# Order of the run-up to sparse attention in a two-layer decoder trunk on one core: compressed-block inner layer in quarters, query norms in halves

## The chip, the cores and the metric

One core of one Trainium2 chip runs the whole program. The metric is device microseconds of one execution, the median of several; lower is better. Engines are named as in the profile: PE (TensorE), PEld (its weight loads), DVE (VectorE), ACT (ScalarE), POOL (GpSimd), SP (SyncE, which issues nearly all transfers).

## What is computed

Two decoder layers on 512 tokens of width 1024. Layer 0 is a retention and mLSTM mixer, layer 1 a sparse attention; a gated MLP with a short convolution and a gated input embedding follow each. The change touches layer 1's attention alone, cut here to what matters:

```python
q = rms_norm(q.reshape(B, T, G, HG, HD), q_g)
def compress(t, pos, w1, w2):
    blk = kv(t)[:, cidx] + pos[:, None, :]
    return jax.nn.gelu(blk @ w1) @ w2
kc = rms_norm(compress(kc, pos_k, w1k, w2k), k_g[0])
vc = compress(vc, pos_v, w1v, w2v)
s = einsum(qq, kc) * scale ; p_c = softmax(s) ; o_cmp = p_c @ vc
p_s = softmax(selected keys)  ; o_slc = p_s @ selected values
p_w = softmax(window keys)    ; o_win = p_w @ window values
o = g0 * o_cmp + g1 * o_slc + g2 * o_win
h = h + o @ w_out ; h = h + conv_ffn(h) ; h = h + gate * rms_norm(p @ ple_w)
```

## The kernel before

Every weight is cut in two float parts, high (`wh`, made by ACT) and low (`wl`, made by DVE), after a 512 KB transfer into `wr`; a product is three matmuls with 512 columns (`mm3`, lines 161 to 163), high by high, low by high, high by low. `load` (line 145) takes each of its three tiles from three buffers in turn: a load's tile waits for the matmuls that read that buffer last, three loads earlier. PSUM has eight banks: four of tag "a", three of "b", one of "o".

The run-up stands at the end of `nsa_mixer`, written out by hand:

- `thin` makes the inputs of the compressed blocks (`hT`) and the gates. `Tokens.steps(c0, c1)` makes the c-th quarter of a product over all tokens: one load and 24 matmuls into four "a" banks. There are three such products: `kv` (keys and values), `q0` (heads 0 to 7), `q1` (heads 8 to 15).
- `blocks` adds positions to `hT` and splits the sums (tiles `xf` and, split, `pt`), for keys on DVE, for values on POOL. `hidden` multiplies them by `w1` in four loads of 16 rows each (lines 803 to 806, eight matmuls of 256 columns a load), adds the halves and applies GELU; `hidden_t` turns the result, `second` multiplies by `w2`, `cmp_keys` norms, `cmp_values` spreads.
- `kv_evac` empties the four `kv` banks; `key_stack` turns one token block of keys (8 transposes, line 772).
- `q_copy` empties two `q` banks (line 869); `q_sums` squares (line 878) and sums (line 880); `q_factor` makes the root by three Newton rounds (lines 204 to 206); `q_norm` multiplies by it (line 902) and splits (lines 896, 900); `q_stack_t` turns four blocks for one head (line 907).
- `Compressed` is the softmax over the compressed blocks for four heads: products (line 930), masked, maxima, shift, exp, factors, scaled, turned.

In source order: `kv` whole, key `hidden` whole, `q0` half, key stacks 0 and 1, `q0` rest with stacks 2 and 3, `q_norm`s, value `hidden` whole, `q1` in pieces, the first four query stacks, `q1` end, `second` for values, first `Compressed` up to its shift. Then 96 attention steps follow (`seq`: 16 heads by 6 units), each a score unit, the probabilities of four steps earlier and the values of two more; a planner (`fits`, `then`) puts other jobs in steps by estimated costs (`PACE` ns a step) and due times: the rest of the first `Compressed`, the squares of `q1`'s queries on POOL (from step 3), the embedding products (`EMBED_AT`).

```python
with tile.TileContext(nc, schedule_with_timeline_sim=True) as tc:
    trunk_kernel(tc, ins, out)
```

This context fixes each engine's queue at build time. It takes instructions by source order as far as they are ready by its own estimates, loads' work ahead (`high_priority`, line 151), so an engine's queue differs from the source. On the chip each queue runs in its order.

Of the kernel before, what the change touches and what calls it, by code (L numbers as in the profile page):

```python
# [20 lines left out]
P = 128  # L21
# [12 lines left out]
LAG, VALUES_LAG, OUT_WAIT = 4, 2, 3  # L34
LAST_AT = (100, 102)
PACE, SLACK = 1800, {"T": 2500, "V": 1000, "S": 1000, "G": 1500}
# [24 lines left out]
class Trunk:  # L61
# [608 lines left out]
    def nsa_mixer(self):  # L670
# [4 lines left out]
        with ExitStack() as ctx:  # L675
# [118 lines left out]
            def hidden(which, xs):  # L794
                ph = self.ps("b")
                for c in range(4):
                    hi, lo = self.load(I["w1"][which, c])
                    for q in range(4):
                        jj = 4 * c + q
                        ws = slice(256 * q, 256 * q + 256)  # L800
                        x = xs[c // 2][:, jj % 8]
                        if jj:
                            nc.tensor.matmul(ph[0:64, 0:256], x[:, 0], lo[:, ws], start=False, stop=False)
                        nc.tensor.matmul(ph[:, 0:256], x.rearrange("p a s -> p (a s)"), hi[:, ws], start=jj == 0, stop=jj == 15)
                        if jj == 0:
                            nc.tensor.matmul(ph[0:64, 0:256], x[:, 0], lo[:, ws], start=False, stop=False)
# [6 lines left out]
            def hidden_t(hid, times):  # L813
# [3 lines left out]
                hh, hl = [self.y()[:, 0 : P * times].rearrange("p (x r b) -> p x r b", x=4, b=32) for _ in range(2)]  # L817
# [70 lines left out]
            def q_norm(zq, r, t, sts, eng):  # L888
                z = zq[t // 2][:, t % 2].rearrange("p (h d) -> p h d", h=8)
                halves = []  # L890
                sts.append(halves)

                def high():
                    halves.extend(self.y().rearrange("p (h a d) -> p h a d", h=4, a=2) for _ in range(2))
                    for c, st in enumerate(halves):
                        nc.scalar.activation(st[:, :, 0], z[:, 4 * c : 4 * c + 4], AF.Copy)

                def low():
                    for c, st in enumerate(halves):
                        eng.tensor_tensor(st[:, :, 1], z[:, 4 * c : 4 * c + 4], st[:, :, 0].bitcast(F32), ALU.subtract)  # L900

                return [lambda: eng.tensor_tensor(z, z, r[:, 8 * t : 8 * t + 8].unsqueeze(2).to_broadcast([P, 8, 64]), ALU.mult), high, low]
# [598 lines left out]
```

## Time and profile before

| | |
|---|---|
| median of 3 runs | 1378.37 us (1378.05 to 1379.83) |
| profiled execution | 1380.31 us, span 1378.6 us, 17917 instructions |
| PE busy | 1361.5 us, 99% of the span |
| DVE, ACT, POOL busy | 832.8, 629.2, 393.9 us |
| run-up, 680 to 780 us | between `kv`'s last quarter and the first attention steps |

The span runs from the first to the last instruction; 1.7 us of the execution lie around it. A row of the timeline gives start, length, engine, line, tile names and, in brackets, idle time before it and what ended that. Matmul lengths overlap: what one costs is the distance between two starts.

### The profile page before, as it was taken

What the parts mean: (1) busy time and instruction counts of PE and PEld (TensorE: products, weight loads), DVE (VectorE), ACT (ScalarE), POOL (GpSimd) and SP (SyncE); (2) the same over time, 40 slices, a digit from 0 to 9 for tenths busy, and PEclk for the clock granted to TensorE, in tenths of its full rate; (3) what the DMA queues carried; (4) which work ended last, traced back from release to release, by engine and by line L of the source; (5) the groups of instructions that cost most, each with busy time, mean ns of one, the idle gap of its engine ahead of it and who ended that gap; (6) DMA issues with size and microseconds to landing.
All of it is one profiled execution on the core that took longest, in us unless ns stands there. A gap on an engine that the chain in (4) does not pass through costs nothing.

```text
span 1378.6 us, 17917 instructions
## 1 busy us (share of the span) xinstructions
PE 1361.5 (99%) x6702; PEld 1123.8 (82%) x6702; DVE 832.8 (60%) x1294; ACT 629.2 (46%) x1086; POOL 393.9 (29%) x392
## 2 busy tenths in 40 slices
PE   9999999999999999999999899999999999999998
PEld 6888788888888888888777678888888888888887
DVE  6765756566356435558766878865766346535555
ACT  5357426444224323336454688774444224313332
POOL 3355502122032101131420696754122022101120
PEclk9999999999999999999999999999999999999999
DMA  6533233233322332233343222012432323233232
GB/s 219 160 93 93 91 107 107 87 97 99 100 92 92 104 95 88 84 123 116 90 142 108 73 74 55 17 50 65 154 107 92 98 97 97 92 100 95 81 110 74
DMA packets 44096, 135.05 MB, mean 98 GB/s; under 512 B 5348, under 2 KB 5988, under 8 KB 44008
## 3 DMA queue, kind: packets, MB, share of 16 engines
q1 hardware_dynamic: 43720, 133.76, 31.2%
q8 instruction: 53, 0.87, 0.3%
q14 instruction: 35, 0.29, 0.1%
q10 hardware_dynamic: 288, 0.14, 0.0%
HBM read 124.69 MB, written 5.25 MB: 94 GB/s over the span
## 4 chain that ended last, share of the span: by engine, by line
PE 91%; DVE 3%; ACT 3%; issue 1%; POOL 1%; DMA 1%; SPq 0%; POOLq 0%; ACTq 0%
PE ps L161 27%; PE ps L163 27%; PE ps L162 26%; PE ps L1037 3%; PE ps L1012 2%; PE ps L981 1%; PE ps L982 1%; PE ps L391 1%; POOL acc L219 1%; DVE wl L134 1%; ACT pr L986 0%; PE ps L256 0%; PE ps L248 0%; PE ps L983 0%; PE ps L459 0%
## 5 line engine op out<-in xcount | busy, mean ns | idle before, releaser
L133 ACT ACTIVATE wh<-wr 128x1024 fp32r<-128x1024 f32 (+2 forms) x216 | 223.3, 1036 | 459.2 <-PE ps L162 366.8
L161 PE MATMUL ps<-y,wh 128*128 128x512 f32 (+1 forms) x1112 | 431.7, 390 | 0.2 <-ACT wh L133 0.2
L162 PE MATMUL ps<-y,wh 128*128 128x512 f32 (+1 forms) x1112 | 430.4, 388 | 0.0
L163 PE MATMUL ps<-y,wl 128*128 128x512 f32 (+1 forms) x1112 | 429.3, 389 | 0.3 <-DVE wl L134 0.3
L134 DVE TENSOR_TENSOR wl<-wr,wh 128x1024 fp32r<-128x1024 f32 (+2 forms) x199 | 246.0, 1237 | 99.3 <-ACT wh L133 98.7
L163 PEld LDWEIGHTS ps<-y,wl 128*128 128x128 f32 x1112 | 208.7, 188 | 44.0 <-DVE wl L134 0.7
L161 PEld LDWEIGHTS ps<-y,wh 128*128 128x128 f32 x1112 | 208.8, 188 | 43.6 <-ACT wh L133 0.7
L162 PEld LDWEIGHTS ps<-y,wh 128*128 128x128 f32 x1112 | 208.9, 188 | 41.8
L1285 POOL TENSOR_TENSOR sc<-sc,rb 128x512 f32<-128x512 f32 x44 | 58.9, 1338 | 469.0 <-ACT sc L1284 469.0
L219 POOL TENSOR_TENSOR acc<-acc,sc 128x512 f32<-128x512 f32 x48 | 75.0, 1562 | 233.4 <-ACT sc L217 230.2
L161 PE MATMUL ps<-gh,wh 128*128 128x512 f32 x352 | 136.9, 389 | 0.0
L162 PE MATMUL ps<-gl,wh 128*128 128x512 f32 x352 | 136.6, 389 | 0.0
L163 PE MATMUL ps<-gh,wl 128*128 128x512 f32 x352 | 136.3, 389 | 0.0
L1300 DVE TENSOR_TENSOR hp<-hp,ps 128x512 f32<-128x512 f32 x48 | 33.0, 687 | 128.3 <-PE ps L163 128.3
L1278 DVE TENSOR_TENSOR a<-ps,rb 128x512 f32<-128x512 f32 x44 | 30.3, 690 | 84.7 <-PE ps L163 84.7
L997 POOL TENSOR_SCALAR pr<-pr,sm,gate 128x512 f32<-128x512 f32 (+3 forms) x128 | 76.8, 619 | 16.5 <-DVE sm L995 11.4
L163 PEld LDWEIGHTS ps<-gh,wl 128*128 128x128 f32 x352 | 66.1, 188 | 13.8
L162 PEld LDWEIGHTS ps<-gl,wh 128*128 128x128 f32 x352 | 66.1, 188 | 13.8
L161 PEld LDWEIGHTS ps<-gh,wh 128*128 128x128 f32 x352 | 66.1, 188 | 13.6
L1286 DVE TENSOR_TENSOR sc<-ps,sc 128x512 f32<-128x512 f32 x44 | 30.3, 688 | 69.1 <-POOL sc L1285 63.9
L986 ACT ACTIVATE pr<-ps,nmx 128x512 f32<-128x512 f32 (+3 forms) x128 | 67.7, 540 | 7.4 <-DVE nmx L984 6.6
L1247 DVE TENSOR_TENSOR pt<-ps,pt 128x512 fp32r<-128x512 f32 (+1 forms) x96 | 56.5, 595 | 19.7 <-ACT pt L1015 19.3
(298 smaller groups left out, 1998.6 us busy)
## 6 DMA issues: line engine op xcount, KB each, us to landing
wr<-in_w_up_dram SPq DMA_DIRECT2D x88, 512.0 KB, 3.6
wr<-in_w_down_dram SPq DMA_DIRECT2D x32, 512.0 KB, 3.5
wr<-in_w_plg_dram SPq DMA_DIRECT2D x16, 512.0 KB, 3.5
wr<-in_w_down_dram SPq DMA_DIRECT2D x16, 384.0 KB, 3.1
hp<-in_xT_dram SPq DMA_DIRECT2D x16, 256.0 KB, 4.1
wr<-in_w_abo_dram SPq DMA_DIRECT2D x8, 512.0 KB, 3.6
wr<-in_w_dram SPq DMA_DIRECT2D x8, 512.0 KB, 3.7
wr<-in_w_q_dram SPq DMA_DIRECT2D x8, 512.0 KB, 3.6
```

Of the source, the lines that this page charges most:

```text
L133: self.nc.scalar.activation(hi, src, AF.Copy)
L134: (eng or self.nc.vector).tensor_tensor(lo, src, hi.bitcast(F32), ALU.subtract)
L161: mm(out, ah, bh, start=first, stop=False)
L162: mm(out, ah, bl, start=False, stop=False)
L163: mm(out, al, bh, start=False, stop=last)
L219: eng.tensor_tensor(n.acc, n.acc, sq, ALU.add)
L986: nc.scalar.activation(pr[:, b], s[:, b], AF.Exp, bias=nmx[:, b : b + 1], accum_out=sm[:, bs[b] : bs[b] + 1])
L997: nc.gpsimd.tensor_scalar(prs[b], prs[b], sm[:, b : b + 1], gate[:, j, hd, 1 + b : 2 + b], ALU.mult, ALU.mult)
L1037: nc.tensor.matmul(po[0:m, cols], vv[i][:, b, g, 0:m], src, start=False, stop=last and b == 1 and i == 0 and part == 0)
L1247: nc.vector.tensor_tensor(*lows, ALU.subtract)
L1285: nc.gpsimd.tensor_tensor(c, c, n.b, ALU.mult)
L1300: nc.vector.tensor_tensor(self.h[m], self.h[m], ps, ALU.add)
```

## The change

The key `hidden` becomes four `hidden_step`s, two among `kv`'s quarters, two among `q0`'s; the value one becomes two pairs around `q1`'s first quarter. Its bank is "o" in place of "b". The normed queries of `q0` get their squares from ACT, straight from PSUM (new line 876 in `q_copy`), in place of DVE; their norms go by halves of four heads, all token blocks of the first half first. Key stacks and the first query stacks move behind the norms. The first `Compressed` goes ahead of `q1`'s second half, and its `exp`, `factors` and `scaled` leave the step planner. The split output of `hidden_t` lies in a `pr` buffer in place of `y`. The first three embeddings take a "b" bank and are copied by DVE in place of ACT. `PACE` is 1950 in place of 1800; the planner looks for room for `q1`'s squares from step 5 in place of 3.

```diff
+Q1_AT = 5
-PACE, SLACK = 1800, ...
+PACE, SLACK = 1950, ...
@@ hidden @@
-            def hidden(which, xs):
-                ph = self.ps("b")
-                for c in range(4):
-                    hi, lo = self.load(I["w1"][which, c])
...
+            def hidden_step(which, xs, ph, c):
+                hi, lo = self.load(I["w1"][which, c])
+                for q in range(4):
...
+            def hidden(ph):
                 hid = self.sc()
@@ q_copy @@
+                    if ss is not None:
+                        sq = self.sc()
+                        nc.scalar.activation(sq, ps[i], AF.Square, scale=r)
+                        nc.vector.tensor_reduce(ss[:, 8 * t : 8 * t + 8], ..., AX, ALU.add)
@@ the run-up @@
-            kv.steps(0, 4)
+            kv.steps(0, 2)
             xk = blocks(0, hT[0])
+            kv.steps(2, 3)
+            ph = self.ps("o")
+            hidden_step(0, xk, ph, 0)
+            kv.steps(3, 4)
+            hidden_step(0, xk, ph, 1)
             keys = kv_evac(kv.ps)
             gate_columns(sg)
-            hk = hidden(0, xk)
             xv = blocks(1, hT[1])
             q0 = self.Tokens(self, I["w_q"][0], n)
-            q0.steps(0, 2)
-            key_stack(0, keys[0])
-            key_stack(1, keys[1])
+            q0.steps(0, 1)
+            hidden_step(0, xk, ph, 2)
+            q0.steps(1, 2)
+            hidden_step(0, xk, ph, 3)
+            hk = hidden(ph)
+            q0.steps(2, 3)
             hkt = hidden_t(hk, 1)
-            q0.steps(2, 3)
-            key_stack(2, keys[2])
-            key_stack(3, keys[3])
             q0.steps(3, 4)
+            zq = [q_copy(q0.ps[0:2], 0, ss), q_copy(q0.ps[2:4], 2, ss)]
+            for f in root + [f for c in range(2) for t in range(NTT) for f in q_norm(zq, r, t, sts, nc.vector, c)]:
+                f()
             po = second(0, *hkt)
             st = cmp_keys(po)
-            ...
-            hv = hidden(1, xv)
+            key_stack(0, keys[0])
+            ph = self.ps("o")
+            hidden_step(1, xv, ph, 0)
+            hidden_step(1, xv, ph, 1)
+            key_stack(1, keys[1])
             q1 = self.Tokens(self, I["w_q"][1], n)
-            q1.steps(0, 2)
-            hvt = hidden_t(hv, 4)
-            cmp_keys_t(st)
-            q1.steps(2, 3)
+            q1.steps(0, 1)
+            key_stack(2, keys[2])
+            hidden_step(1, xv, ph, 2)
+            hidden_step(1, xv, ph, 3)
+            hv = hidden(ph)
+            key_stack(3, keys[3])
             for hd in range(4):
                 q_stack_copy(hd, q_stack_t(sts, hd, "b"))
+            q1.steps(1, 2)
+            cmp_keys_t(st)
+            comp = Compressed(0, "b")
+            for f in (products, masked, comp.maxima, comp.shift, comp.exp, comp.factors, comp.scaled):
+                f()
+            with self.behind(nc.tensor):
+                hvt = hidden_t(hv, 4)
+                q1.steps(2, 3)
+            cmp_values(second(1, *hvt))
             q1.steps(3, 4)
-            cmp_values(second(1, *hvt))
-            comp = Compressed(0, "b")
```

Where the queues change at the places that the prediction speaks of:

DVE at the last quarter of `kv` (before; `wl_903` and `wl_906` are `kv`'s quarters 2 and 3, counted from 0, `wl_923` is the first quarter of the key `w1`, `xf` the position sums):

```order
L134 TENSOR_TENSOR wl_903_5318<-wr_901_5316,wh_902_5317 128x1024
L715 TENSOR_TENSOR sc_885_5221<-ps_874_5138,rb_883_5214 128x512
L715 TENSOR_TENSOR sc_886_5223<-ps_878_5169,rb_883_5214 128x512
L134 TENSOR_TENSOR wl_906_5348<-wr_904_5346,wh_905_5347 128x1024
L789 TENSOR_TENSOR xf_907_5376<-sc_885_5221,cols_76 64x8x31
L185 TENSOR_TENSOR sc_890_5247<-sc_890_5247,ps_889_5230 64x512
L789 TENSOR_TENSOR xf_907_5376<-sc_885_5221,cols_76 64x8x31 x7
L722 TENSOR_TENSOR sc_890_5247<-sc_890_5247,rb_883_5214 48x512
L134 TENSOR_TENSOR wl_923_5456<-wr_921_5454,wh_922_5455 128x1024
```

The same place now (`wl_906` is quarter 2, `wl_910` the first of `w1`, `wl_913` is `kv`'s quarter 3; lines are those of the changed file):

```order
L135 TENSOR_TENSOR wl_906_5335<-wr_904_5333,wh_905_5334 128x1024
L716 TENSOR_TENSOR sc_885_5221<-ps_874_5138,rb_883_5214 128x512
L716 TENSOR_TENSOR sc_886_5223<-ps_878_5169,rb_883_5214 128x512
L135 TENSOR_TENSOR wl_910_5366<-wr_908_5364,wh_909_5365 128x1024
L790 TENSOR_TENSOR xf_901_5316<-sc_885_5221,cols_76 64x8x31
L186 TENSOR_TENSOR sc_890_5247<-sc_890_5247,ps_889_5230 64x512
L790 TENSOR_TENSOR xf_901_5316<-sc_885_5221,cols_76 64x8x31 x7
L723 TENSOR_TENSOR sc_890_5247<-sc_890_5247,rb_883_5214 48x512
L135 TENSOR_TENSOR wl_913_5380<-wr_911_5378,wh_912_5379 128x1024
```

`kv`'s quarter 3 and the first quarter of `w1` have changed places around the position sums.

ACT at the value `hidden` (before; `wh_1001` is the last quarter of the value `w1`, `wh_1009` to `wh_1030` the four quarters of `q1`):

```order
L133 ACTIVATE wh_1001_5871<-wr_1000_5870 128x1024
L133 ACTIVATE wh_1009_5893<-wr_1008_5892 128x1024
L133 ACTIVATE wh_1012_5923<-wr_1011_5922 128x1024
L808 ACTIVATE sc_1003_5884<-ps_990_5827 64x256
L133 ACTIVATE wh_1019_5964<-wr_1018_5963 128x1024
L810 ACTIVATE sc_1003_5884<-sc_1003_5884 64x256
L133 ACTIVATE wh_1030_6022<-wr_1029_6021 128x1024
```

And now (`wh_1002` and `wh_1005` are the third and fourth quarter of the value `w1`, `wh_1020` is `q1`'s second quarter, the `y` rows are high parts of normed queries, line 896 before):

```order
L134 ACTIVATE wh_1002_5877<-wr_1001_5876 128x1024
L911 ACTIVATE y_966_5701<-ep_957_5663 128x4x64
L911 ACTIVATE y_967_5705<-ep_960_5672 128x4x64
L911 ACTIVATE y_968_5709<-ep_960_5672 128x4x64
L134 ACTIVATE wh_1005_5891<-wr_1004_5890 128x1024
L911 ACTIVATE y_969_5713<-ep_957_5663 128x4x64
L911 ACTIVATE y_970_5717<-ep_957_5663 128x4x64
L134 ACTIVATE wh_1020_5955<-wr_1019_5954 128x1024
```

The query norms now stand among these splits; they stood behind them.

DVE at the first attention steps (before; `sc_1034` is the first `Compressed`, `nmx` the maximum of a score unit, `vc` the compressed values):

```order
L861 TENSOR_TENSOR sc_1033_6064<-ps_1032_6051,sc_1033_6064 128x64
L863 TENSOR_TENSOR vc0_5114<-sc_1033_6064,rows4_5116 128x512
L861 TENSOR_TENSOR sc_1033_6064<-ps_1032_6051,sc_1033_6064 128x64
L935 TENSOR_TENSOR sc_1034_6071<-ps_1037_6074,maskc_5038 128x256
L863 TENSOR_TENSOR vc1_5115<-sc_1033_6064,rows4_5116 128x512
L936 TENSOR_TENSOR sc_1034_6071<-sc_1034_6071,ps_1037_6074 128x256
L935 TENSOR_TENSOR sc_1034_6071<-ps_1038_6083,maskc_5038 128x256
L984 TENSOR_REDUCE nmx_1050_6120<-ps_1053_6123 128x1
L936 TENSOR_TENSOR sc_1034_6071<-sc_1034_6071,ps_1038_6083 128x256
L984 TENSOR_REDUCE nmx_1055_6137<-ps_1057_6139 128x1
```

And now (`tiny_1047` are sums of squares of `q1`, whose squares POOL makes; `y_1059` is the first embedding):

```order
L863 TENSOR_TENSOR sc_1035_6070<-ps_1034_6057,sc_1035_6070 128x64
L865 TENSOR_TENSOR vc0_5114<-sc_1035_6070,rows4_5116 128x512
L863 TENSOR_TENSOR sc_1035_6070<-ps_1034_6057,sc_1035_6070 128x64
L865 TENSOR_TENSOR vc1_5115<-sc_1035_6070,rows4_5116 128x512
L888 TENSOR_REDUCE tiny_1047_6126<-sc_1094_6267 128x8
L888 TENSOR_REDUCE tiny_1047_6126<-sc_1101_6293 128x8
L888 TENSOR_REDUCE tiny_1047_6126<-sc_1108_6320 128x8
L1000 TENSOR_REDUCE nmx_1050_6129<-ps_1053_6132 128x1
L1372 COPY y_1059_6158<-ps_1054_6138 128x512
L888 TENSOR_REDUCE tiny_1047_6126<-sc_1119_6364 128x8
L1000 TENSOR_REDUCE nmx_1055_6145<-ps_1057_6147 128x1
```

`Compressed` is gone from here (it stands before `q1`'s third quarter); three sums of squares stand ahead of the first score maximum, and an embedding copy behind it.

## Rows read from the trace of the kernel before

**Rows 1.** The page's head: span, and busy time of the engines

```profile
span 1378.6 us, 17917 instructions
PE 1361.5 (99%) x6702; PEld 1123.8 (82%) x6702; DVE 832.8 (60%) x1294; ACT 629.2 (46%) x1086; POOL 393.9 (29%) x392
```

**Rows 2.** Stretches: length, busy PE, PEld, DVE, ACT, POOL, granted clock, DMA share, GB/s

```profile
690.00:700.00 10.00, 9.12 (x47) 7.55 (x48) 8.21 (x21) 5.58 (x7) 0.00 (x0) 1.00 0.61 208
...
720.00:730.00 10.00, 7.40 (x40) 5.94 (x39) 9.61 (x17) 5.24 (x11) 0.00 (x0) 0.89 0.45 129
730.00:740.00 10.00, 10.00 (x43) 7.90 (x42) 9.64 (x38) 5.03 (x13) 0.00 (x0) 0.94 0.50 160
...
760.00:770.00 10.00, 8.91 (x48) 6.10 (x45) 9.93 (x29) 8.50 (x25) 7.45 (x11) 1.00 0.25 91
770.00:780.00 10.00, 6.80 (x38) 5.33 (x36) 8.38 (x17) 5.18 (x12) 8.74 (x9) 0.83 0.27 79
...
800.00:960.00 160.00, 159.01 (x1102) 133.03 (x1101) 114.02 (x249) 117.32 (x333) 106.39 (x143) 1.00 0.18 49
```

**Rows 3.** PE's timeline at its three losses; in brackets idle before, and its end

```profile
690.82 0.33 PE L803 MATMUL ps<-wl,pt 128*64 128x256 f32 x1 [2.14 <-DVE wl L134]
...
725.60 0.33 PE L803 MATMUL ps<-wl,pt 128*64 128x256 f32 x1 [1.28 <-DVE wl L134]
...
775.12 0.45 PE L981 MATMUL ps<-hp,y 128*128 128x384 f32 x1 [2.45 <-DVE y L913]
```

**Rows 4.** PE's timeline, `kv`'s last quarter: first and last of its 24 matmuls

```profile
680.65 0.39 PE L161 MATMUL ps<-wh,y 128*128 128x512 f32 x1
...
685.87 0.39 PE L163 MATMUL ps<-wh,y 128*128 128x512 f32 x1
```

**Rows 5.** DVE's timeline: splits of `w1`'s first and second quarter

```profile
681.98 1.21 DVE L134 TENSOR_TENSOR wl<-wr,wh 128x1024 fp32r<-128x1024 f32 x1
...
689.54 1.22 DVE L134 TENSOR_TENSOR wl<-wr,wh 128x1024 fp32r<-128x1024 f32 x1
```

**Rows 6.** PE's timeline: 16 matmuls of `hidden`, first and last; eight transposes

```profile
707.66 1.04 PE L772 MATMUL ps<-ident,st 128*128 128x128 f32 x8
...
720.41 0.28 PE L803 MATMUL ps<-wl,pt 128*64 128x256 f32 x1
...
722.11 0.28 PE L804 MATMUL ps<-wh,pt 128*128 128x256 f32 x1
```

**Rows 7.** ACT's timeline: two weight splits, eight query splits, two copies

```profile
658.13 2.01 ACT L133 ACTIVATE wh<-wr 128x1024 fp32r<-128x1024 f32 x2 [2.19 <-PE ps L162]
...
734.96 2.57 ACT L896 ACTIVATE y<-ep 128x256 fp32r<-128x256 f32 x8
...
746.62 0.58 ACT L915 ACTIVATE y<-ps 128x512 fp32r<-128x512 f32 x1
747.09 0.27 ACT L853 ACTIVATE kc<-ps 128x128 fp32r<-128x128 f32 x1
```

**Rows 8.** DVE's groups by shape, 655 to 790 us: busy us, mean ns, idle before

```profile
L863 DVE TENSOR_TENSOR vc<-sc,rows 128x512 fp32r<-128x512 f32 x2 | 3.6, 1822 | 0.0
...
L913 DVE CAST y<-ps 128x512 fp32r<-128x512 f32 x4 | 2.8, 689 | 5.2 <-PE ps L907 5.2
...
L935 DVE TENSOR_TENSOR sc<-ps,maskc 128x256 f32<-128x256 f32 x4 | 1.6, 412 | 0.0
L936 DVE TENSOR_TENSOR sc<-sc,ps 128x256 f32<-128x256 f32 x4 | 1.5, 408 | 0.0
```

**Rows 9.** DVE's timeline: a Newton operation, twice; POOL's: a weight split

```profile
732.60 0.26 DVE L204 TENSOR_TENSOR tiny<-tiny 128x32 f32<-128x32 f32 x2
...
772.20 1.81 DVE L204 TENSOR_TENSOR tiny<-tiny 128x32 f32<-128x32 f32 x1
...
771.61 2.36 POOL L143 TENSOR_TENSOR wl<-wr,wh 128x1024 fp32r<-128x1024 f32 x1
```

**Rows 10.** POOL's groups by shape, 655 to 790 us: squares of `q1`

```profile
L878 POOL TENSOR_TENSOR sc<-ep 128x512 f32<-128x512 f32 x4 | 4.9, 1262 | 0.0
```

More of the change, by code (lines that the diff above doesn't have):

```diff
@@ L34 @@
 LAG, VALUES_LAG, OUT_WAIT = 4, 2, 3
+Q1_AT = 5
 LAST_AT = (100, 102)
-PACE, SLACK = 1800, {"T": 2500, "V": 1000, "S": 1000, "G": 1500}
+PACE, SLACK = 1950, {"T": 2500, "V": 1000, "S": 1000, "G": 1500}
 EMBED_AT = (0, 1, 2, 6, 12, 17, 22, 27)
@@ L886, in q_factor, with q_norm, scaled @@
                 return r, [mean] + root + [scale]
[L888 removed]
+            def q_norm(zq, r, t, sts, eng, half=None):
+                cs = (0, 1) if half is None else (half,)
                 z = zq[t // 2][:, t % 2].rearrange("p (h d) -> p h d", h=8)
[L890 to L891 removed]
+                hs = slice(4 * cs[0], 4 * cs[-1] + 4)
+                if t == len(sts):
+                    sts.append([None, None])
+                def scaled():
+                    rb = r[:, 8 * t + hs.start : 8 * t + hs.stop].unsqueeze(2).to_broadcast([P, hs.stop - hs.start, 64])
+                    eng.tensor_tensor(z[:, hs], z[:, hs], rb, ALU.mult)
                 def high():
[L894 to L895 removed]
+                    for c in cs:
+                        st = sts[t][c] = self.y().rearrange("p (h a d) -> p h a d", h=4, a=2)
                         nc.scalar.activation(st[:, :, 0], z[:, 4 * c : 4 * c + 4], AF.Copy)
                 def low():
[L899 removed]
+                    for c in cs:
+                        st = sts[t][c]
                         eng.tensor_tensor(st[:, :, 1], z[:, 4 * c : 4 * c + 4], st[:, :, 0].bitcast(F32), ALU.subtract)
[L902 removed]
+                return [scaled, high, low]
             def q_stack_t(sts, hd, tag):
@@ L1122, in nsa_mixer @@
             ew = [self.load(I["w_ple"][1, 0])]
-            seq = [(hd, *u) for hd in range(16) for u in UNITS]
             todo, load = defaultdict(list), {e: defaultdict(int) for e in "TVSG"}
@@ L1192, in embed @@
                 got = []
-                then(s0, ("T", 1360, lambda: got.append(emb.products(m, ew[m // 4]))), ("S", 600, lambda: emb.keep(m, got[0])))
+                then(s0, ("T", 1360, lambda: got.append(emb.products(m, ew[m // 4], "b" if s0 < LAG else "a"))), ("V" if s0 < LAG else "S", 650, lambda: emb.keep(m, got[0], s0 < LAG)))
             def out_first(m, s0):
@@ L1199, in nsa_mixer @@
             wo = {}
-            for step, e, n, f in ((0, "S", 630, comp.exp), (1, "V", 1100, comp.factors), (2, "G", 1050, comp.scaled), (4, "T", 440, comp.turned), (5, "S", 600, comp.high), (6, "V", 690, comp.low)):
+            for step, e, n, f in ((1, "T", 440, comp.turned), (2, "S", 600, comp.high), (3, "V", 690, comp.low)):
                 load[e][step] += n
@@ L1208, in nsa_mixer @@
                 a, b = q_sums(zq, ss1, t, nc.gpsimd)
-                last = max(last, then(3 + t, ("G", 1050, a), ("V", 690, b)))
+                last = max(last, then(Q1_AT + t, ("G", 1050, a), ("V", 690, b)))
             for k in (0, 4, 7):
@@ L1330, in inputs, with products @@
             self.p = [x.rearrange("p (k t) -> p k t", k=2) for x in self.k.load(self.k.I["pT"][self.i])]
-        def products(self, m, w):
-            ps = self.k.bank()
+        def products(self, m, w, tag=None):
+            ps = self.k.ps(tag) if tag else self.k.bank()
             for k in range(2):
```

47 lines of the change are left out of this document (24 added, 23 removed).

## The prediction

> **What bounds the kernel.** The page's head first: PE is busy 1361.5 of 1378.6 us [rows 1], and the change keeps PE's instructions, 6746 matmuls before and after. So it can gain only time in which PE stands still or runs below its full clock, and these lie, for the places that the change touches, between 685 and 780 us. The stretches show them [rows 2]: PE idle 10.00 − 7.40 = 2.60 in 720 to 730, 10.00 − 8.91 = 1.09 in 760 to 770, 10.00 − 6.80 = 3.20 in 770 to 780. With the 2.14 before 690.82 [rows 3] that is 9.03 us. The clock is granted at 0.89, 0.94 and 0.83 in three stretches of 10 us [rows 2], at 1.2 GHz for a part of them and 2.4 for the rest: (0.11 + 0.06 + 0.17) × 10 = 3.4 us of full-speed work. It falls behind the losses near 725 and 775; after the 2.14 at 690 it stays 1.00 [rows 2, 3]. In all **12.4 us**. Behind 800 us PE idles 0.99 in 160 us [rows 2], so nothing is to be had there.
>
> The bracketed waits say why [rows 3]. Two follow a low split of a `w1` quarter on DVE (2.14, 1.28): in `hidden` a load feeds only eight matmuls, while a quarter of `kv` feeds 24 at (685.87 − 680.65)/23 = 0.227 us, 5.4 us [rows 4]. Sixteen matmuls of `hidden` take (722.11 − 720.41) × 16/15 = 1.8 [rows 6], 0.9 for a load, less than the 1.21 of one low split on DVE [rows 5]. Four such loads in a row outrun DVE, and the change puts each one or two between longer pieces. The third wait is 2.45 for the copy of a query stack (line 913) at the loop's start, where DVE is busy 9.93 + 8.38 = 18.3 of 20 us [rows 2, 3].
>
> **The change part by part.**
>
> *Removed: 12.4 us.* The two `w1` waits go, since the rows that fed them no longer stand together; the loop-start wait goes as far as DVE is relieved there (D). The clock's 3.4 goes if no loss of the size of those at 725 and 775 comes back.
>
> *A: `kv`'s quarter 3, +1.6.* Its low split stands on DVE behind the position sums, where the first `w1` split stood (order above). Thus it starts about 681.98 and ends at 683.19 [rows 5]. PE starts that quarter's high products about 680.65 and wants its low part at the fifth matmul, 680.65 + 4 × 0.227 = 681.56 [rows 4]. Wait 683.19 − 681.56 = 1.6. Behind the split on DVE stand the second `w1` split and the evacuations of `kv`; PE then has 16 matmuls of `hidden` and the rest of `kv` before it wants the banks, which covers them. Bounds 0 (if DVE reaches it early) and 1.6.
>
> *B: query splits among weight splits on ACT, +1.2.* From the third value load to `q1`'s second quarter, ACT holds three weight splits of 1.0 (2.01 for two) and five query splits of 2.57/8 = 0.32 [rows 7]: 4.6 us. PE has meanwhile two loads of `hidden` at 0.9 and twelve transposes at 1.04/8 = 0.13 [rows 6], 3.4 us. The difference is 1.2. If all eight query splits come late it is 3.0 + 2.57 − 3.4 = 2.2; if they are done early, 0. I take the middle because the order has five of them between.
>
> *C: `Compressed` ahead of `q1`'s second half, +0.6.* Its first product waits on ACT for a weight split (1.0), a stack copy (0.58) and `kc` (0.27) [rows 7], 1.85 us, against ten transposes at 0.13 [rows 6], 1.3. The difference is 0.6; without that cover 1.9, and 0 if the split is early. In exchange the shift and exponentials lie under 48 matmuls.
>
> *D: the loop's start, +1.2 in place of 1.09 + 3.20 = 4.3.* DVE's queue there loses the two `vc` spreads, 3.6, which come earlier, and half of eight maskings, (1.6 + 1.5)/2 = 1.6 [rows 8]; it gains three embedding copies, priced as the copy of a 128x512 bank at line 913, 3 × 0.69 = 2.1 [rows 8]. Relief 3.1, so 4.3 − 3.1 = 1.2 stays. Bounds 0 and 4.3: whether the relief falls before the late copy, no row shows.
>
> *At nothing.* The squares of `q0` on ACT add four operations there and take four from DVE; they run bank by bank while PE makes 6 × 0.227 = 1.4 us of products for each bank [rows 4], and one copy takes 0.58 [rows 7], two 1.2. If that cover fails, `q1`'s first quarter waits for a bank, some tenths of a us, within B's bounds. The `pr` buffer, the "o" bank and the norm by halves change places alone. Loads keep their number; DMA is at most 0.61 busy in these stretches [rows 2], so SP's changed order of transfers costs nothing. On POOL the squares of `q1` stand before the first step's scalings as before, so `Q1_AT` moves little. `PACE` moves jobs in a loop that idles 0.99 in 160 us.
>
> *Sum.* 1.6 + 1.2 + 0.6 + 1.2 = 4.6 added, 12.4 removed: −7.8. On the profiled execution, 1380.31 − 7.8 = 1372.5; this stands 1.94 above the median of 1378.37, so **1370.6** for the median. Two tenths of a per cent, 2.8 us, are about what a measurement of this kernel can tell from no change; under 1375.6 counts as faster. Within this case A alone gives −10.8, **1367.6**.
>
> **The rivals.**
>
> *R1, the clock falls once more.* Waits B, C or D lie close together and the clock goes down behind them as after 725 and 775. Half of 3.4 is 1.7 a fall: 1372.3, with two falls 1374.0. For it: losses of 2.6 and 3.2 did it. Against: 2.14 did not [rows 2, 3], and each new wait is under that.
>
> *R2, DVE and POOL hold each other up at the loop's start.* A Newton operation (line 204) took 0.26 for two at 732.60 and 1.81 for one inside a POOL weight split of 2.36 us [rows 9]. Nine such operations (three rounds of lines 204 to 206) for `q1` still lie among POOL's scalings and splits, now with embedding copies between, so the relief of D may be eaten. Then D is 4.3 and one fall of the clock stays: 4.3 − 1.2 + 1.7 = 4.8 more, 1375.4. The Trainium skill (SBUF — State Buffer, section "Who interferes with whom") says that a VectorE instruction with two SBUF inputs contends with a GpSimd instruction that reads SBUF, through a shared port pair held by one of them for a whole instruction; by that rule the second would wait out the first, and the 1.81 against the 0.26 agrees with it [rows 9].
>
> *R3, the waits only change places.* All at their upper ends: 1.6 + 2.2 + 1.9 + 4.3 = 10.0, and one fall 1.7: 11.7 against 12.4, 1377.7, no change. For it: ACT and DVE keep all their work, and DVE is over 9 of 10 us busy through much of this part [rows 2].
>
> *R4, slower: the first score maximum is held by POOL.* On DVE three sums of squares now stand ahead of the first maximum and an embedding copy behind; before, the first two maxima stood ahead of them (order above). Each sum waits for a POOL square of 4.9/4 = 1.26 [rows 10], and the exponentials, probabilities and score banks wait for the maximum. If POOL starts its squares only when PE starts scores, 3 × 1.26 = 3.8 comes on top of the three copies, 2.1, and the old 4.3: D is 10.2. With A to C (3.4) and the clock as before (3.4) that is 17.0 against 12.4: +4.6, **1383.0**. It decides from the point where POOL's third square ends later than PE's embedding and score products ahead of the first probabilities last. Against it: the squares can follow the bank copies one by one while `q1`'s last quarter still runs.
>
> *R5, the change does not do what it says* can be left out: the order shows the pieces interleaved.
>
> **How the numbers follow.** Forecast 0.45, R1 0.18, R2 0.14, R3 0.13, R4 0.10. The likeliest is 1370.6, its own range 1367.6 to 1373. The range from 1367.6 to 1378 takes in R1, R2 and R3; outside remain R4 and some part of unnamed losses, under 0.2. Faster: forecast, R1 and a bit over half of R2 (it lies at the border), 0.45 + 0.18 + 0.08 = 0.71. Same: the rest of R2 and most of R3, 0.06 + 0.11 = 0.17. Slower: R4 and the upper edge of R3, 0.12.
>
> **What would show it.** In the changed profile: a PE wait of some 1.6 on DVE's `wl` inside `kv`'s quarter 3; about 1 us on ACT's `wh` at `q1`'s second quarter; about half a us on `kc` before the first `Compressed` products; the stretch that holds value `hidden` at clock 1.00 and PE nearly full; at the loop's start under 2 us idle. Wrong: the clock below 1.00 in more than one stretch of 10 us (R1, R2), a wait over 3 us at the first probabilities whose chain leads to DVE's sums and POOL's squares (R4), or a wait of over 2 us at a place not named here.

## The result, and the profile after

The changed kernel takes **1370.2 us** (median of 6 runs, 1368.64 to 1371.78) against 1378.5 before (6 runs, 1378.05 to 1380.42). The ratio is 0.9936, 95% interval 0.9923 to 0.9949: faster by 8.3 us, where 7.8 were forecast. The profiled execution took 1369.42 us. One execution of a later version, e10, that took 1452.83 us at a mean granted clock of 0.88 is a slow one and left out below.

The page's head, to hold against [rows 1]:

```profile
span 1367.7 us, 17941 instructions
...
PE 1355.7 (99%) x6702; PEld 1121.7 (82%) x6702; DVE 831.7 (61%) x1297; ACT 630.1 (46%) x1087; POOL 401.1 (29%) x392
```

The same work on every engine but for a handful of instructions, and POOL 7.2 us busier with the same 392; one instruction, shown under e5, explains most of that. The stretches, columns as in [rows 2]:

```profile
680.00:690.00 10.00, 8.47 (x44) 6.86 (x43) 9.85 (x15) 7.80 (x14) 4.80 (x5) 1.00 0.34 101
...
720.00:730.00 10.00, 9.13 (x63) 7.96 (x62) 10.00 (x37) 7.58 (x20) 4.72 (x1) 1.00 0.25 74
730.00:740.00 10.00, 8.22 (x52) 6.85 (x49) 6.73 (x12) 6.11 (x13) 1.37 (x1) 1.00 0.66 209
...
760.00:770.00 10.00, 10.00 (x71) 8.56 (x71) 9.85 (x31) 9.10 (x26) 7.49 (x11) 1.00 0.36 125
770.00:780.00 10.00, 10.00 (x72) 8.13 (x72) 6.58 (x16) 6.92 (x23) 10.00 (x13) 1.00 0.30 92
```

PE is full from 740 to 780, where 4.3 us were lost before [rows 2], and the granted clock is 1.00 in every stretch from 680 to 800 us. PE's waits, from its timeline:

```profile
683.66 0.50 PE L163 MATMUL ps<-wl,y 128*128 128x512 f32 x1 [1.53 <-DVE wl L135]
...
726.40 0.34 PE L803 MATMUL ps<-wl,pt 128*64 128x256 f32 x1 [0.22 <-DVE wl L135]
...
728.22 1.20 PE L162 MATMUL ps<-wh,y 128*128 128x512 f32 x4 [0.66 <-ACT wh L134]
...
731.42 0.66 PE L773 MATMUL ps<-ident,st 128*128 128x128 f32 x4 [1.07 <-POOL st L767]
...
739.38 1.97 PE L946 MATMUL ps<-kc,y 128*128 128x64 f32 x16 [0.71 <-ACT kc L855]
...
781.35 0.39 PE L997 MATMUL ps<-hp,y 128*128 128x256 f32 x1 [0.18 <-ACT pr L1002]
...
942.12 1.21 PE L162 MATMUL ps<-y,wh 128*128 128x512 f32 x4 [0.91 <-ACT y L134]
```

Up to 739 these are waits A (1.53), B (0.22 and 0.66), one that was not foreseen (1.07) and C (0.71): 4.19 us in all. Before, there were 2.14, 0.74, 1.28 and 0.58, 4.74 in all (two of them in [rows 3]); so the waits of the run-up became only 0.55 shorter. The waits of the loop's start are down to 0.18, and one of 0.91 is new, at the products behind the attention (942.12).

Where the time came from is read between two points that both traces have, PE's first score product and ACT's first square of the norm behind the attention. Before:

```profile
754.56 0.48 PE L981 MATMUL ps<-hp,y 128*128 128x512 f32 x1
...
958.01 0.61 ACT L217 ACTIVATE sc<-hp 128x512 f32<-128x512 f32 x1
```

After:

```profile
755.07 0.39 PE L997 MATMUL ps<-hp,y 128*128 128x512 f32 x1
...
947.12 0.61 ACT L218 ACTIVATE sc<-hp 128x512 f32<-128x512 f32 x1
```

The first score starts 0.5 us later, though PE has by then done more: by the order of the two programs 5 more matmuls of 512 columns (0.227 each, [rows 4]) and 14 more products of `Compressed` (1.97 us for 16 in the row above), 2.8 us in all. So the run-up gained some 2.3 us; the layer's norm began 0.4 later, too (659.60 in place of 659.16), which makes it 2.7. From the first score to the norm it took 203.45 us before and 192.05 now; less the 2.8 moved out, the loop gained 8.6. The two profiled executions are 10.9 apart, more than the medians (8.3): the one of before was among the longer of its kernel, the one of after among the shorter of its own. So these stages tell where time was gained, and the medians how much on the whole.

### The profile page after: what moved, and what is told of

It is laid out like the page before. It is cut to its first block, busy times and chain, and to the rows that moved or that the text cites. A ratio compares the mean times of both kernels' runs of the same rounds, so it can differ in the third digit from the quotient of the medians.

```text
span 1367.7 us, 17941 instructions
## 1 busy us (share of the span) xinstructions
PE 1355.7 (99%) x6702; PEld 1121.7 (82%) x6702; DVE 831.7 (61%) x1297; ACT 630.1 (46%) x1087; POOL 401.1 (29%) x392
## 4 chain that ended last, share of the span: by engine, by line
PE 95%; DVE 1%; ACT 1%; POOL 1%; issue 0%; DMA 0%; SPq 0%; POOLq 0%; ACTq 0%
PE ps L162 27%; PE ps L164 27%; PE ps L163 27%; PE ps L1053 3%; PE ps L1028 2%; PE ps L997 1%; PE ps L998 1%; PE ps L392 1%; PE ps L999 1%; POOL acc L220 1%; PE ps L946 1%; PE ps L257 0%; PE ps L249 0%; PE ps L460 0%; DVE xf L790 0%
## 5 line engine op out<-in xcount | busy, mean ns | idle before, releaser
L1314 ACT ACTIVATE sc<-sc 128x512 f32<-128x512 f32 x44 | 27.8, 632 | 85.2 <-DVE sc L1313 85.0
```

## The experiments

Each kernel is the changed one with the edit shown in short form, unless it says otherwise; times are medians, and the ratio in brackets has its 95% interval. The runs were made in three groups on three chips, each with the kernel before beside them (medians 1380.2 for e1 to e4, 1379.9 for e5 to e8, 1378.5 for e9 to e12). An interval is some 1.8 us to either side, so two versions that differ by less than that are told apart by their traces and not by their times. The traces are compared by the two stages used above, and a table behind e12 has them for every version: the run-up, from the norm's first product on PE (line 249; 248 before) to the first score, and the loop, from there to the first square of the norm behind the attention. What lies behind that square takes 420.5 to 420.6 us in all fourteen.

**e1, the key hidden layer in a row.**

```diff
-kv.steps(2, 3); hidden_step(0, xk, ph, 0); kv.steps(3, 4); hidden_step(0, xk, ph, 1)
+kv.steps(2, 4)
 keys = kv_evac(kv.ps); gate_columns(sg)
+for c in range(4): hidden_step(0, xk, ph, c)
-q0.steps(0, 1); hidden_step(0, xk, ph, 2); q0.steps(1, 2); hidden_step(0, xk, ph, 3)
+q0.steps(0, 3)
```

> The changed kernel, but with the four loads of the key hidden layer in a row behind kv, as before the change. Theory (what counts are the PE waits that a piece makes): the wait of 1.53 us inside kv's quarter 3 goes, the wait of about 2.1 for the low split of w1's second quarter comes back; no fall of the clock; net +0.6, 1370.8 us. Rival (interleaving itself is worth its whole removed wait, since the wait of 1.53 has another cause, the position sums on DVE): both waits are there, +2.1, 1372.3 us.

Measured 1370.49 us, ratio 0.9934 (0.9921 to 0.9946). The 1.53 is gone, and in its place stands 2.12 at the second quarter of `w1`:

```profile
689.84 0.33 PE L803 MATMUL ps<-wl,pt 128*64 128x256 f32 x1 [2.12 <-DVE wl L135]
```

The theory holds in the trace: interleaving the key layer exchanges one wait for a shorter one. The waits behind it shift as well (0.22 becomes 0.85, 1.07 becomes 0.54), and the run-up is 1.1 us longer. In the medians the 0.3 us are within what can be told.

**e2, the value hidden layer in a row**, ahead of `q1`.

```diff
 hidden_step(1, xv, ph, 0)
 hidden_step(1, xv, ph, 1)
+hidden_step(1, xv, ph, 2)
+hidden_step(1, xv, ph, 3)
+hv = hidden(ph)
 key_stack(1, keys[1])
 q1.steps(0, 1)
 key_stack(2, keys[2])
-hidden_step(1, xv, ph, 2)
-hidden_step(1, xv, ph, 3)
-hv = hidden(ph)
```

> The changed kernel, but with the four loads of the value hidden layer in a row ahead of q1, as before the change. Theory: the waits on weight splits around it come back (0.74, 1.28 and 0.58 us before, 0.22 and 0.66 now: +1.7), lie within 5 us of each other, and the granted clock falls below 1.00 there for some 1.7 us of work: +3.4 in all, 1373.6 us. Rival (the squares of q0 on ACT and the norms by halves have already taken the load off DVE there, and the interleaving does nothing): the same time, 1370.2 us, clock 1.00.

Measured 1368.67 us, ratio 0.9918 (0.9905 to 0.9932): the theory falls. No wait on a weight split of the value layer comes back. PE's waits near it are now

```profile
716.83 0.63 PE L773 MATMUL ps<-ident,st 128*128 128x128 f32 x4 [1.26 <-issue]
...
717.71 0.39 PE L804 MATMUL ps<-wh,pt 128*128 128x256 f32 x1 [0.25 <-ACT sc L837]
```

one at a key stack and one on ACT's reading of `second`. The profile names no releaser for the first; it ends 0.10 behind ACT's second copy out of the "b" bank that was taken three turns earlier (716.34 + 0.39 = 716.73), so it is put down to that bank. The waits of 0.66 on a high split and of 1.07 on POOL are gone, and the run-up is 1.0 us shorter. The pieces around `q1`'s first quarter gain nothing.

**e3, the first `Compressed` at its old place** (behind `q1`, its exponentials in the planner's steps).

```diff
-comp = Compressed(0, "b"); products, masked, maxima, shift, exp, factors, scaled
 q1.steps(2, 3); cmp_values(second(1, *hvt)); q1.steps(3, 4)
+comp = Compressed(0, "b"); products, masked, maxima, shift
-for ... in ((1, "T", 440, comp.turned), ...
+for ... in ((0, "S", 630, comp.exp), (1, "V", 1100, comp.factors), (2, "G", 1050, comp.scaled), (4, "T", 440, comp.turned), ...
```

> The changed kernel, but with the first Compressed behind q1 and second, its exponentials, factors and scaling in the planner's steps as before the change. Theory: the wait of 0.71 us on kc goes and the waits at the loop's start come back (0.39, 0.42, 0.74 and 2.45 before, 0.18 now: +3.8), with a fall of the clock of 1.7: +4.8 in all, 1375.0 us. Rival 1 (DVE is relieved enough by the other parts): within 1 us of 1370.2. Rival 2 (the embedding copies on DVE, on top of the late maskings, make it worse than before the change): over 5 us at the loop's start, 1377 us.

Measured 1372.85 us, ratio 0.9950 (0.9937 to 0.9962). The loop's waits are back, and the stretches show that the clock did not follow:

```profile
762.22 0.66 PE L1028 MATMUL ps<-ident,pr 128*128 128x128 f32 x4 [1.07 <-POOL pr L1013]
...
767.46 0.66 PE L975 MATMUL ps<-ident,sc 128*128 128x128 f32 x4 [1.80 <-POOL sc L970]
...
771.55 0.45 PE L997 MATMUL ps<-hp,y 128*128 128x384 f32 x1 [2.25 <-DVE y L929]
```

```profile
760.00:770.00 10.00, 6.27 (x38) 4.43 (x36) 9.86 (x24) 6.75 (x20) 8.15 (x10) 1.00 0.22 84
770.00:780.00 10.00, 8.45 (x68) 7.42 (x69) 8.51 (x23) 6.63 (x20) 8.11 (x11) 1.00 0.26 79
```

5.3 us of PE's 20 are idle at clock 1.00. So the wait part of the theory holds and its clock part does not; the theory's 1375.0 less the 1.7 for the clock is 1373.3, close to what came. The place of `Compressed` is worth 2.7 us by the medians (1.9 by the ratios) and 4.4 by the two stages of the traces.

**e4, the planner's two numbers as before.**

```diff
-Q1_AT = 5
+Q1_AT = 3
-PACE, SLACK = 1950, ...
+PACE, SLACK = 1800, ...
```

> The changed kernel, but with the planner's two numbers as before the change (PACE 1800, squares of q1 looked for from step 3). Theory (the loop had nothing to give): 1370.2 us within 1 us. Rival (the trace of the changed kernel has some 3 us less of short gaps under 0.2 us between PE's instructions in 800 to 860 us, and the wider steps did that): they come back, 1373 us, with no wait over 1 us that is new.

Measured 1371.55 us, ratio 0.9944 (0.9932 to 0.9957), between the two. PE waits in the loop, where the changed kernel has none between the 0.18 at its start and the 0.91 at its end (the three longest):

```profile
815.20 0.39 PE L1053 MATMUL ps<-pt,vv 128*64 128x128 f32 x2 [0.29 <-DVE pt L1277]
...
837.18 0.44 PE L997 MATMUL ps<-ep,y 128*128 128x384 f32 x1 [0.55 <-ACT pr L1002]
...
841.32 0.50 PE L1040 MATMUL ps<-y,vc 128*128 128x512 f32 x1 [0.98 <-ACT sc L1063]
```

The wait of 0.91 behind the attention goes in exchange. By the medians the numbers bring 1.4 us (1.1 by the ratios), which time alone does not tell from nothing. The traces show more: the same run-up (95.44 and 95.47), and a loop of 195.43 in place of 192.05, 3.4 longer. Of that PE is idle for 1.6 and busy for 1.8 longer over the same 1334 matmul records (192.75 in place of 190.96). The profiled execution of the changed kernel began its norm 1.3 later, so the two are only 2.1 apart as a whole. The forecast had the numbers at nothing. The two were not tried apart.

**e5, squares of `q0` on DVE and norms by whole blocks.**

```diff
-zq = [q_copy(q0.ps[0:2], 0, ss), q_copy(q0.ps[2:4], 2, ss)]
+zq = [q_copy(q0.ps[0:2], 0), q_copy(q0.ps[2:4], 2)]
-for f in root + [... for c in range(2) for t in range(NTT) for f in q_norm(zq, r, t, sts, nc.vector, c)]:
+steps = [f for t in range(NTT) for f in q_sums(zq, ss, t, nc.vector)] + root
+for f in steps + [... for t in range(NTT) for f in q_norm(zq, r, t, sts, nc.vector)]:
```

> The changed kernel, but with the squares of q0's queries on DVE and the norms one token block after the other, as before the change; the value hidden layer stays in two pairs. Theory N (formed after e2: the weight waits near the value hidden layer left because 4 x 0.62 us of squares left DVE, and the interleaving does nothing): the waits of 1.28 and 0.58 us come back, 1372 us. Rival (either the interleaving or the relief of DVE is enough by itself): within 1 us of 1370.2.

Measured 1367.24 us, ratio 0.9911 (0.9898 to 0.9925): faster than the changed kernel, which neither had expected: its four runs (1366.75 to 1367.41) all lie below the six of the changed kernel (1368.64 to 1371.78). Theory N falls. Its waits in the run-up are 1.53, 0.48, 0.73 and 0.37, together 3.11 us in place of 4.19; the one of 1.07 is gone. In the changed kernel POOL's timeline has the same cast twice:

```profile
719.40 0.43 POOL L767 CAST st<-st 128x256 fp32r<-128x256 f32 x1 [12.44 <-DVE st L766]
725.27 6.09 POOL L767 CAST st<-st 128x256 fp32r<-128x256 f32 x1 [5.44 <-DVE st L766]
```

0.43 us, and then 6.09 (6.09 or 6.10 in the traces of e3, e4, e7 and e12 too). DVE at that time (first and last row of the queue over it; 10.00 of 10 us busy in 720 to 730):

```profile
725.14 1.21 DVE L135 TENSOR_TENSOR wl<-wr,wh 128x1024 fp32r<-128x1024 f32 x1
...
731.03 0.40 DVE L843 SCALAR_TENSOR_TENSOR sc<-sc,tiny,gains 64x64 f32<-64x64 f32 x1
```

It runs weight splits and query splits, operations with two operands in SBUF, with hardly a gap, and the key stack's cast ends only at 731.36; PE's transposes of it start at 731.42. In the changed kernel the cast's input, the low part of the key stack (line 766), is made on DVE in the middle of the norm; in e5 it is made ahead of it, and the cast takes its usual time. DVE's row in the changed kernel, in e5, and the cast in e5:

```profile
724.80 0.41 DVE L766 TENSOR_TENSOR st<-sc,st 128x256 fp32r<-128x256 f32 x1
...
718.99 0.42 DVE L766 TENSOR_TENSOR st<-sc,st 128x256 fp32r<-128x256 f32 x1
...
719.48 0.40 POOL L767 CAST st<-st 128x256 fp32r<-128x256 f32 x1 [0.55 <-DVE tiny L841]
```

The run-up is 1.5 us shorter than the changed kernel's. The medians differ by 3.0, and part of the rest is the clock: its mean was 1.000 in all four runs, 0.9988 over the changed kernel's six, which is 1.6 us (a thousandth of the time is 1.4). The edit undoes two things, the squares on ACT and the norm by halves; which of them places the cast badly was not tried.

**e6, both undone**: the edits of e2 and e5 together.

> Both undone: value hidden layer in a row (as e2) and squares and norms as in e5. Theory N: against e2 the waits of 0.74, 1.28 and 0.58 us are back, with a fall of the clock in part of the runs: 1368.7 + 2.6 = 1371.3 us, up to 1373. Rival (the key stacks that now stand ahead of the value hidden layer cover its weight splits, whoever makes the squares): within 1 us of e2, 1368.7.

Measured 1369.41 us, ratio 0.9926 (0.9912 to 0.9940). The rival's number holds: PE waits 0.68 at a key stack and 0.79 for ACT ahead of the value layer, and not once for its weights. Its cause, the key stacks, is put to the test in e9. Together the two edits gain no more than either alone (1368.67 and 1367.24).

**e7, the first embeddings in "a" banks, copied by ACT.**

```diff
-emb.products(m, ew[m // 4], "b" if s0 < LAG else "a") ... ("V" if s0 < LAG else "S", 650, ...)
+emb.products(m, ew[m // 4]) ... ("S", 600, ...)
```

> The changed kernel, but with the first three embeddings in the banks of tag a and copied by ACT, as before the change. Theory (in the changed trace no loss stands at the loop's start, so the place of three copies of 0.69 us is hidden): within 1 us of 1370.2. Rival (the copies on DVE pay, as ACT is at its limit in 780 to 790 us of the changed trace, 10.00 busy of 10): waits on ACT of 1 to 2 us at the loop's start, 1371.5 us.

Measured 1371.0 us, ratio 0.9934 (0.9922 to 0.9947): within 1 us, as the theory says; the one new wait near the loop's start is 0.26. The two stages together are 0.9 longer.

**e8, from e2: the key layer later, compressed keys turned earlier.**

```diff
-hidden_step(0, xk, ph, 0); kv.steps(3, 4); hidden_step(0, xk, ph, 1)
+kv.steps(3, 4); hidden_step(0, xk, ph, 0)
-q0.steps(0, 1); hidden_step(0, xk, ph, 2); q0.steps(1, 2); hidden_step(0, xk, ph, 3); hk = hidden(ph); q0.steps(2, 3)
+q0.steps(0, 1); hidden_step(0, xk, ph, 1); q0.steps(1, 2); hidden_step(0, xk, ph, 2); q0.steps(2, 3); hidden_step(0, xk, ph, 3); hk = hidden(ph)
+cmp_keys_t(st)
 for hd in range(4): q_stack_copy(hd, q_stack_t(sts, hd, "b"))
 q1.steps(1, 2)
-cmp_keys_t(st)
```

> From e2, with two waits attacked: kv's quarter 3 is loaded ahead of w1's first quarter again and the other three pieces of the key hidden layer stand behind q0's quarters 0, 1 and 2; the turn of the compressed keys stands ahead of the query stacks. Theory (each named PE wait is worth its length): the waits of 1.53 and 0.66 us go, 1368.7 - 2.2 = 1366.5 us. Rival (kv's four banks are not emptied in time for q0, as only one piece of 0.9 us stands between): a wait of 1 to 2 us at q0's first products, 1368 us.

Measured 1370.24 us, ratio 0.9930 (0.9918 to 0.9943), 1.6 us above e2; the run-up is 2.6 longer than e2's (97.11 and 94.48). The 1.53 and the 0.66 go as the theory has it, but the key layer now ends too late for `second`, and the clock falls, there and once more 30 us later, where PE is full:

```profile
712.83 0.33 PE L818 MATMUL ps<-ident,sc 64*128 64x64 f32 x2 [0.73 <-ACT sc L812]
...
715.66 0.24 PE L162 MATMUL ps<-w,pr 128*64 128x64 f32 x1 [1.47 <-ACT pr L134]
```

```profile
710.00:720.00 10.00, 7.38 (x42) 6.27 (x41) 6.44 (x21) 9.26 (x21) 0.43 (x1) 0.84 0.41 144
...
740.00:750.00 10.00, 10.00 (x49) 8.46 (x48) 4.64 (x10) 3.79 (x5) 2.10 (x2) 0.83 0.12 46
```

The rival named the wrong wait (no bank of `kv` was late).

**e9, from e6: key stacks among `q0`'s products again.**

```diff
+key_stack(0, keys[0]); key_stack(1, keys[1])
 q0.steps(2, 3)
 hkt = hidden_t(hk, 1)
+key_stack(2, keys[2]); key_stack(3, keys[3])
```

> From e6 (value hidden layer in a row, squares and norms as before the change), with the key stacks back among q0's products as well. Theory K (formed after e6: what covers the weight splits of the value hidden layer is the 32 transposes of the key stacks, which the change puts ahead of and around it): the waits of 1.28 and 0.58 us on low splits and of 0.74 on a high split come back in place of e6's 0.68 and 0.79, and the clock falls in most runs: 1371.5 to 1373 us. Rival (the last run's order of ACT and DVE is better by chance, whatever covers it): within 1 us of e6, 1369.4.

Measured 1370.19 us, ratio 0.9935 (0.9922 to 0.9949): Theory K falls. PE waits 1.73 us ahead of the value layer for ACT's reading of `second`, and by then the weights are there:

```profile
719.78 0.39 PE L804 MATMUL ps<-wh,pt 128*128 128x256 f32 x1 [1.73 <-ACT sc L837]
```

Whether the key stacks would cover the weights where this wait is absent, e9 does not show.

**e10, from e5**: the key layer's second and third piece behind `q0`'s quarter 0, its fourth behind quarter 1 (so that it ends where it did), the turn as in e8.

> From e5 (the fastest so far): kv's quarter 3 ahead of w1's first quarter again, the key hidden layer's other pieces behind q0's quarters 0 (two pieces) and 1 (one), so that it ends where it does in the changed kernel; the turn of the compressed keys ahead of the query stacks. Theory: waits of 1.53, 0.73 and 0.37 us go, 1367.2 - 2.6 = 1364.6 us. Rival (as in e8, the second product waits for the key hidden layer's GELU and its turn, 2.6 us in all, and the clock falls): 1367 us or more.

Measured 1364.85, 1366.93 and 1367.75 us, ratio 0.9911 (0.9896 to 0.9926): no better than e5 by what the times can tell. In its trace the waits are gone as expected, and its run-up is 2.0 us shorter than e5's (91.91 and 93.94); but the three runs' mean granted clocks are 0.999, 0.999 and 0.997, where e5 has 1.000 in all four. By the times, e5 and e10 are the fastest versions of this study.

**e11, the change's second half alone, on the kernel before**: run-up up to `q1` as before (the value and key layers in a row in a "b" bank, and the keys' `second` ahead of the norms again), then the changed part.

> The kernel before, with the change's second half alone: q1's quarters, the first Compressed and its exponentials ahead of q1's end, embedding copies on DVE, the planner's two numbers. Both hidden layers in a row, key stacks, squares and norms as before. Theory: the waits of 2.14, 1.28, 0.58 and 0.74 us stay with a fall of the clock of 1.7; those at the loop's start (0.39, 0.42, 0.74, 2.45), their fall of 1.7 and some 1.4 in the loop go, with 0.7 on kc and 0.9 behind the attention added: 1379 - 5.5 = 1373.5 us. Rival (without the first half's relief of DVE the tail brings nothing): 1378 us.

Measured 1374.9 us, ratio 0.9973 (0.9961 to 0.9984). The waits on the weights of both hidden layers are back:

```profile
689.89 0.34 PE L803 MATMUL ps<-wl,pt 128*64 128x256 f32 x1 [2.15 <-DVE wl L135]
...
724.70 0.33 PE L803 MATMUL ps<-wl,pt 128*64 128x256 f32 x1 [1.27 <-DVE wl L135]
```

**e12, the first half alone**: the edits of e3, e4 and e7 together.

> The changed kernel without that second half: the first Compressed at the loop's start, embedding copies on ACT in banks of tag a, PACE 1800, squares from step 3. The hidden layers in pieces, squares on ACT, norms by halves and key stacks as in the changed kernel. Theory (effects add): 1370.2 + 2.7 (e3) + 1.4 (e4) + 0.8 (e7) = 1375 us. Rival (the undone parts are each other's cover, and the losses at the loop's start come in full with the clock's fall): 1377 us.

Measured 1374.66 us, ratio 0.9972 (0.9960 to 0.9983). The halves bring 0.27 and 0.28 of the 0.64%: within the intervals they add. Of e12's waits, two at the loop's start and the longest of the loop:

```profile
766.02 0.66 PE L975 MATMUL ps<-ident,sc 128*128 128x128 f32 x4 [1.26 <-POOL sc L970]
...
769.21 0.44 PE L997 MATMUL ps<-hp,y 128*128 128x384 f32 x1 [1.34 <-DVE y L929]
...
820.01 0.63 PE L1028 MATMUL ps<-ident,pr 128*128 128x128 f32 x4 [0.85 <-DVE pt L1277]
```

The stages of the profiled executions, in us:

| version | run-up | loop | both |
|---|---|---|---|
| before | 95.40 | 203.45 | 298.85 |
| changed | 95.47 | 192.05 | 287.52 |
| e1, key layer in a row | 96.56 | 192.01 | 288.57 |
| e2, value layer in a row | 94.48 | 192.03 | 286.51 |
| e3, first `Compressed` late | 93.63 | 198.26 | 291.89 |
| e4, planner's numbers | 95.44 | 195.43 | 290.87 |
| e5, squares and norms | 93.94 | 192.02 | 285.96 |
| e6, e2 and e5 | 94.83 | 192.01 | 286.84 |
| e7, embeddings | 94.85 | 193.56 | 288.41 |
| e8, e2 with the key layer later | 97.11 | 192.02 | 289.13 |
| e9, e6 with key stacks early | 95.52 | 192.03 | 287.55 |
| e10, e5 with the key layer later | 91.91 | 192.05 | 283.96 |
| e11, second half alone | 102.33 | 192.03 | 294.36 |
| e12, first half alone | 93.56 | 200.14 | 293.70 |

Each is one execution. Before the first score PE has 2.8 us less work in the kernel before than in the changed one, and some 1.1 less in e3, e7 and e12, so for these only the last column compares like with like. It orders the versions much as the medians do.

The last two rows say more than the sum of the halves. The second half by itself already brings the loop to its full shortness, 192.03. But without the first half its run-up, less the 2.8 of work moved into it, is 4.1 us longer than before the change: the weight waits stand, three waits behind them are new (0.85, 0.47, 0.37), and the clock falls to 0.66 in a stretch of 10 us (shown at the end). So in the changed kernel the first half keeps the run-up from paying for the loop.

## Why the prediction was right, point by point

- **What was removed.** The low-split waits named at the two hidden layers (2.14, 1.28) and those at the loop's start went. The clock's part went in the profiled pair, 0.997 before and 1.000 now. Over all runs it is smaller: the kernel before ran at a mean of 0.9974 in the 29 runs beside the experiments, the changed one at 0.9988 in 6. That is 1.4 thousandths or 2.0 us, where the sum has 3.4: most executions of the changed kernel still lose some of it.
- **A, 1.6 us.** Measured 1.53, at the place, matmul and engine named (the row at 683.66).
- **B, 1.2 us.** Measured 0.22 + 0.66 = 0.88, on both splits. ACT's timeline has the order that was named: three query splits between the third and the fourth value split, two behind that, and then the split of `q1`'s second quarter, which ends at 728.17, 0.05 ahead of PE's start at 728.22. No experiment moves these splits alone.
- **C, 0.6 us.** Measured 0.71 on `kc`; ACT makes a weight split, a stack copy and `kc` in a row ahead of it (737.61 to 739.32), as the sum has it. e8 and e10, which turn the keys earlier, have no such wait.
- **D, 1.2 us.** Measured 0.18. Here the relief was sized too small: not the old 4.3 less 3.1 of DVE work was what remained, but nearly nothing. e3 shows why: with `Compressed` back, the waits go to POOL's scaling of it (1.80) and to the queue behind it on DVE (2.25). The chain over POOL had to leave, and not DVE's microseconds alone. The embedding copies, charged to DVE with 2.1, show no such cost: PE waits for none of them, and with the copies back on ACT the kernel is no faster (e7).
- **At nothing: `q0`'s squares on ACT.** This step failed, together with the norm by halves, which stood at nothing beside it. e5 without both is 0.25% faster. The cover was argued for ACT's banks, and no such wait for a bank shows; but with the two edits the norm's splits run on DVE while POOL casts a key stack, and PE waits 1.07 for that cast, a wait that no part of the sum had.
- **At nothing: `PACE`.** With `Q1_AT`, this failed the other way: 3.4 us in the traces, 1.4 in the medians (e4). The 0.99 us of idle time in 160 [rows 2] was taken for all that the loop could give. By the two points above the loop gained 8.6 us. Of this 0.39 + 0.42 + 0.74 + 2.45 − 0.18 = 3.8 are waits at its start, 1.7 the clock; with the two waits of before at 820 and 851 (0.43 and 0.21) and the new 0.91 that makes 5.3. Shorter gaps bring 0.6 (PE idles 5.27 us in the loop before and 1.09 now). The other 2.7 stand in PE's busy time, 198.18 before and 190.96 now, less the 2.8 that moved and the clock's 1.7: matmuls that start further apart without the profile calling PE idle. They were not followed one by one, but e4 has 1.8 of the same kind, so the planner's numbers can account for most of them.
- **The sum.** Run-up: forecast 2.14 + 2.60 + 1.7 − 3.4 = 3.0, measured 2.7. Loop: forecast 4.8, measured 8.6 in the profiled pair. In the medians the whole is 8.3 for 7.8 forecast. In the profiled pair the two stages gain 11.3, 3.5 more than forecast; over the medians less of this shows, in good part because the clock's share is 2.0 there and not 3.4. So the mechanisms A, B and C were right in place and size, and that the total came within 0.5 us is in part luck: a loss that was missed (1.07) and a clock term that was too large stand against gains in the loop that were missed.
- **The rivals.** R1 did not come in the profiled execution; five of the six runs have means of 0.997 to 0.999, and where their clock fell no trace shows. R2's mechanism came, at another place, in the cast of 6.09 us beside 0.43. The Trainium skill (SBUF — State Buffer, section "Who interferes with whom") says that a VectorE instruction with two SBUF inputs contends with a GpSimd instruction that reads SBUF; the 6.09 agrees with that. R3 came in the run-up alone, where 4.19 us of waits stand in place of 4.74. R4 did not come: no wait near the first scores is over 0.18.
- **Within the run-up** the parts do not add. Undoing the key layer (e1), the value layer (e2), the norms (e5) or the key stacks besides (e9) costs at most 0.3 us each by the medians, and 1.1 by the traces. All of them together cost 4.7 and 6.9 (e11 against the changed kernel); e11 also moves the keys' `second` ahead of the norms again and the layers back to a "b" bank. In e2, e6 and e9 waits of 1.5 to 1.7 us in all, at a key stack or for ACT's reading of `second`, stand ahead of the value layer, and its weights are ready behind them; in e11 `second` stands earlier and both weight waits are back. So the place of `second` may be what covers the weights there; no run moves it alone, and which single edit would be enough stays open.

## What to carry to other kernels

Price a wait at the place where it stands, and expect another to take its place: in the run-up most waits only changed their name (4.74 us became 4.19), and what paid in the loop was taking a chain over three engines out of a stretch where all were full, and wider steps in the planner. Undo each part of a change that helped: one pair of edits here cost 0.25%. The granted clock of the one profiled execution (1.000) is not that of the others (0.997 to 0.999). A list of waits is a lower bound for what an engine loses, since 2.7 us here stood in busy time; where jobs are spread over a loop by estimated costs, try the estimates.

## What the runs showed of the hardware that was not expected

- A POOL cast of 128x256 took 6.09 us in place of 0.43, while DVE ran operations with two SBUF operands with hardly a gap; it came out at 6.09 or 6.10 in all five traces with this order, and at 0.40 in e2 and e5, where its input is made ahead of that queue (2.14 in e1, where it starts later in it). The forecast had reckoned with a hold of one operation (1.81 for one of them, [rows 9]), and here it outlasted more than ten.
- The granted clock did not follow the size of the loss. It stayed 1.00 over 5.3 idle us of 20 (e3), and fell to 0.84 in a stretch of 10 with 2.6, and to 0.83 in one without any (e8). In e11 it was 1.00 over the losses of 720 to 740 and fell behind them:

```profile
720.00:730.00 10.00, 7.38 (x41) 5.85 (x40) 9.29 (x17) 4.98 (x8) 0.00 (x0) 1.00 0.54 156
730.00:740.00 10.00, 8.84 (x42) 6.47 (x40) 10.00 (x41) 5.11 (x12) 0.00 (x0) 1.00 0.51 162
740.00:750.00 10.00, 9.16 (x38) 7.59 (x38) 6.29 (x12) 3.71 (x6) 1.05 (x1) 0.66 0.17 52
```

So the prediction's sentence that it falls behind losses of a certain size was not borne out; what decides it is not settled here.
